# A decoder layer on one core: the pool mixer's bias for half of the token tiles is added by accumulating transfers instead of products

## The chip, the cores and the metric

The kernel runs on one core of one Trainium2 chip. The metric is the time on the device in microseconds (us). A core has five engines that run at the same time, each its own instructions in order: TensorE (PE in the profile, with weight loads as PEld), VectorE (DVE), ScalarE (ACT), GpSimd (POOL) and SyncE (SP). Transfers between memories are issued by an engine and carried out by 16 DMA engines; those that GpSimd issues are queue q0 of the profile, those that SyncE issues are q1. GpSimd's transfers can also add what they bring to what stands at the destination; such a transfer is called accumulating here.

## The reference

One layer with the mixer of kind 0 is computed, for 1024 tokens and a width of 1024, all in float32:

```python
h = rms_norm(x, norm_mix_g)
y = pool_mixer(h, pool_w, pool_b, pool_scale)
x = x + y
f = conv_ffn(rms_norm(x, norm_ffn_g), ffn_w_in, ffn_conv_w, ffn_conv_b, ffn_w_out)
x = x + f
```

`pool_mixer` subtracts h from causal means over 2, 4, 8 and 16 tokens (one window for each quarter of the columns), multiplies each quarter by its own 256 x 256 weights, adds the bias `pool_b` and multiplies by `pool_scale`, one number a column. So the term `pool_scale * pool_b` is one row of 1024 numbers that is added to every token. `conv_ffn` multiplies by a 1024 x 5632 matrix, convolves over three tokens, gates, and multiplies by a 2816 x 1024 matrix.

## The kernel before

**Mixer.** The 1024 tokens are eight tiles j = 0 to 7 of 128 tokens (one a partition) by 1024 columns. For each tile, `rstd_of` on ScalarE takes the norm (`junk_a`, line 178), VectorE scales the band matrix with it (`bandr`, line 187), and TensorE makes the window sums out of the tile as it was loaded (`psd`, line 201). VectorE adds the part that comes from the tile before (line 270), ScalarE copies the result into SBUF as `dh` (line 271), and TensorE multiplies it by the pool's weights, which already hold gain and scale (`psy`, line 286). The bias follows as two products with ones into the same bank (line 289): `bias_hl` holds the bias row, split into two float32r parts in its first two partitions and zero elsewhere, and `ones` is a 128 x 128 tile of ones. VectorE adds the tile `xs[j]` to the bank (line 292), in place, which gives the tile after the mixer, x1; SyncE stores it to `x1_dram`. Its norm follows (`junk_b`), VectorE makes the normed tile `n` (line 304), and TensorE transposes it (`pst`, line 319) into the operand of the feed-forward part. The PSUM banks of `psd`, `psy` and `pst` come from one pool of three, in the order of their use.

**Feed-forward.** Both large products are done by a scheme of seven half-size products (P1 to P7, `STEPS` at line 405), each made from sums and differences of quarters of the operands, and each operand is split into two float32r parts by ScalarE and VectorE (`split`, lines 91 and 92). For a column tile n, `load_in` brings 128 x 2048 numbers `win n` with the quarters a11, a12, a21 and a22. Four sums of the quarters are operands: S1 = a21 + a22 in the place of a21, S2 = a11 + S1 in that of a11, S4 = a12 + S2 in that of a12, and S3 = a11 + a21 in a tile of its own, for which SyncE loads a11 a second time (line 366). Where time allows, `sums_in` makes these by accumulating transfers on GpSimd's queue (line 361); for the column tiles 0 and 1 it makes all four so, during the mixer.

**Order.** The order on each engine is written out by hand: the loop at line 527 runs the tiles in a skewed way (in pass j the norm of tile j, the windows of tile j - 1, the output of tile j - 2, the transposes of tile j - 4), and `issue_after` puts an instruction behind another on its engine. It starts the first products of the feed-forward part among the last tiles. Every engine, GpSimd's queue too, takes its instructions strictly in that order, so a transfer whose wait isn't over holds up all that are behind it.

The loop's passes call these for the sums of column tiles 0 and 1:

```python
if j in (4, 6):
    load_in(j // 2 - 2)
    sums_in(j // 2 - 2, 0)
...
if j in (7, 8):
    sums_in(j - 7, 1)
```

Of the kernel before, what the change touches and what calls it, by code (L numbers as in the profile page):

```python
# [7 lines left out]
F32 = mybir.dt.float32  # L8
# [3 lines left out]
ALU = mybir.AluOpType  # L12
PSUM = bass.MemoryType.PSUM

P = 128
S = 1024
D = 1024
# [22 lines left out]
NOPS_A = 3  # L40

XBUFS = 5

PAD = 24

# [18 lines left out]
def trunk_kernel(ctx: ExitStack, tc: tile.TileContext, x, consts, par, rows, pool_w, w_in, w_out, out):  # L64
    nc = tc.nc

    const = ctx.enter_context(tc.tile_pool(name="const", bufs=1))
    dram = ctx.enter_context(tc.tile_pool(name="dram", bufs=1, space=bass.MemoryType.DRAM))
# [4 lines left out]
    work = ctx.enter_context(tc.tile_pool(name="work", bufs=1, side="right"))  # L73
# [6 lines left out]
    def bank2(name):  # L80
        return ps_p.tile([P, 2 * NH], F32, tag="ps", name=name)
# [16 lines left out]
    xs = {}  # L98

    def load_x(j):  # L100
        if j < 2 or j >= 2 + XBUFS:
            xs[j] = hls.tile([P, D], F32, tag="hl", name=f"x{j}", bufs=7)
        else:
            xs[j] = pp.tile([P, D], F32, tag="x", name=f"x{j}", bufs=XBUFS)
        for cols in HALVES if j == 0 else [slice(0, D)]:
            nc.sync.dma_start(xs[j][:, cols], x[j * P : (j + 1) * P, cols])
# [28 lines left out]
    for g, w in enumerate(WINDOWS):  # L135

        m = band[:, g, :]
# [56 lines left out]
    def mixer_norm(j):  # L194
        t = bands[j] = pp.tile([P, NG, P], F32, tag="bandr", name=f"bandr{j}", bufs=2)
        for groups in [slice(0, 2), slice(2, 4)] if j == 0 else [slice(0, NG)]:
            marks[f"band{j}"] = normed(t[:, groups, :], (band if j else band0)[:, groups, :], stats[j])

    def windows(ps, src, weights):
        for c in range(NK):  # L200
            m = nc.tensor.matmul(ps[:, c * P : (c + 1) * P], src[:, c * P : (c + 1) * P], weights[:, c // 2, :], start=True, stop=True)  # L201
        return m.ins
# [13 lines left out]
    wps = pp.tile([P, 2 * NG, GRP], F32, tag="wps", name="wps")  # L216
# [13 lines left out]


    b8 = rows8[:, 1, :]

    def pool_bias():
        marks["bias"] = nc.scalar.activation(bias8[:, 0, :], b8, AF.Copy).ins
        marks["bias_dve"] = nc.vector.tensor_tensor(bias8[:, 1, :], b8, bias8[:, 0, :].bitcast(F32), ALU.subtract).ins
        for l in range(2):
            m = nc.sync.dma_start(bias_hl[l : l + 1, :].bitcast(F32), bias8[:, l, :].bitcast(F32)).ins
        with tc.issue_after(m):
            for j in range(3, NS):  # L240
                load_x(j)
            nc.sync.dma_start(par_sb[:, :GM], par[:, :GM])
# [14 lines left out]
    def window_sums(j):  # L257
        ps = bank2(f"psd{j}")
        marks[f"psd{j}"] = windows(ps, xs[j], bands.pop(j))
        return ps  # L260

    def mixer_window(j, ps=None):
        ps = window_sums(j) if ps is None else ps
        dh = ds[j] = pp.tile([P, NK, P], F32, tag="dh", name=f"dh{j}", bufs=2)
        ps3 = ps.rearrange("p (c s) -> p c s", c=NK)
        first = ps3[:, :, :HALO]
        if j == 0:
            marks["first"] = nc.vector.tensor_tensor(first, first, fac, ALU.mult).ins
        elif j > 1:
            nc.vector.tensor_tensor(first, first, edges[:, :, j * HALO : (j + 1) * HALO], ALU.add)  # L270
        marks[f"dh{j}"] = nc.scalar.activation(dh, ps3, AF.Copy).ins
# [9 lines left out]
    def mixer_out(j, stats=True):  # L281
        dh = ds.pop(j)
        ps = bank2(f"psy{j}")
        for c in range(NK):
            o = ps[:, c // 2 * GRP : (c // 2 + 1) * GRP]
            nc.tensor.matmul(o, dh[:, c, :], wps[:, c, :], start=c % 4 == 0, stop=False, skip_group_check=True)  # L286
        for h in range(2):
            cols = slice(h * NH, (h + 1) * NH)
            m = nc.tensor.matmul(ps[:, cols], ones, bias_hl[:, cols], start=False, stop=True, skip_group_check=True)  # L289
        marks[f"psy{j}"] = m.ins  # L290
        x1 = n2s[j] = xs.pop(j)
        marks[j] = nc.vector.tensor_tensor(x1, ps, x1, ALU.add).ins
        nc.sync.dma_start(x1_dram[j * P : (j + 1) * P, :], x1)
        if stats:
            mixer_out_stats(j)

    def mixer_out_stats(j):
        n2s[j] = (n2s[j], rstd_of(n2s[j], f"b{j}"))

    def ffn_norm(j):  # L300
        x1, r = n2s[j]
        n2 = n2s[j] = pp.tile([P, D], F32, tag="n2", name=f"n2_{j}", bufs=2)
        nc.vector.tensor_tensor(r[1], r[0], r[1], ALU.mult)
        marks[f"n{j}"] = nc.vector.scalar_tensor_tensor(n2, x1, r[1], gains[0], op0=ALU.mult, op1=ALU.mult).ins
# [10 lines left out]
    def ffn_operand(j):  # L315
        n2 = n2s.pop(j)
        ps = bank2(f"pst{j}")
        for c in range(NK):
            nc.tensor.transpose(ps[:, c * P : (c + 1) * P], n2[:, c * P : (c + 1) * P], ident)  # L319
        ps3 = ps.rearrange("p (c a s) -> p c a s", c=NK, a=2)  # L320
        lo, hi = slice(0, 4), slice(4, 8)
        half, q = divmod(j, NS // 2)
        cols = slice(q * P // 2, (q + 1) * P // 2)
        here, first = (n2f[:, :, h * NH : (h + 1) * NH].rearrange("p c (a s) -> p c a s", a=2)[:, :, :, cols] for h in (half, 0))
        if half == 0:
            split_n(nops["B11"], ps3[:, lo], cols)
            split_n(nops["B21"], ps3[:, hi], cols)
            nc.scalar.activation(here, ps3, AF.Copy)
            return
        b11, b12, b22 = first[:, lo], ps3[:, lo], here[:, hi]  # L330
        nc.scalar.activation(b22, ps3[:, hi], AF.Copy)
        sub(b11, b11, b12)
        marks["T1"] = split_n(nops["T1"], b11, cols)
        sub(here[:, lo], b22, b12)
# [20 lines left out]
    def tmp(name):  # L355
        return work.tile([P, NH], F32, tag="sum", name=name, bufs=3)

    def sums_in(n, step):

        def more(out, a):  # L360
            nc.gpsimd.dma_start(out, a, accum_op=ALU.add)

        a11, a12, a21, a22 = (raws[n][:, i, k * NH : (k + 1) * NH] for i in range(2) for k in range(2))
        if step == 0:
            s3 = sums[n, "S3"] = tmp(f"S3_{n}")
            nc.sync.dma_start(s3, w_in[order[n]][:, 0, :NH])
            more(s3, a21)
            more(a21, a22)
        else:
            sums[n, "S2"] = a11  # L370
            more(a11, a21)
            sums[n, "S4"] = a12
            more(a12, a11)
# [95 lines left out]
    def prep_event(k):  # L469
        if k < len(events):  # L470
            n, p = events[k]
            prep_in(n, STEPS[p][0])
# [49 lines left out]
        mixer_edges()  # L522
    with tc.issue_after(marks["edges_pe"]):
        sums3 = window_sums(3)
    with tc.issue_after(marks["dh1+"]), tc.issue_after(marks["edges"]):
        mixer_out_stats(0)
    for j in range(2, NS + 4):
        if 3 < j < NS:
            with tc.issue_after(marks[1]) if j == 4 else nullcontext():
                mixer_norm(j)  # L530
        if 1 <= j - 1 < NS and j > 2:
            mixer_window(j - 1, {3: sums2, 4: sums3}.get(j))
        if j == NS + 1:
            with tc.issue_after(marks[f"n{NS - 2}"]):
                prep_event(4)
                prep_event(6)
        if 1 <= j - 2 < NS:
            with tc.issue_after(marks["S4", 0] if j == NS + 1 else marks[f"band{min(j, 4)}"]) if j > 2 else nullcontext(), tc.issue_after(marks["psd3"]):
                mixer_out(j - 2)
        if 0 <= j - 2 < NS:  # L540
            with tc.issue_after(marks["dh1+"]):
                ffn_norm(j - 2)
        if 0 <= j - 4 < NS:
            ffn_operand(j - 4)
        if j in (4, 6):
            load_in(j // 2 - 2)
            sums_in(j // 2 - 2, 0)
        if 5 <= j <= 8:
            with tc.issue_after(marks[j - 2]), tc.issue_after(marks[f"b{j - 3}"]):
                prep_event(j - 5)  # L550
        if j in (7, 8):
            sums_in(j - 7, 1)
        if j in (8, 10, 11):
            event((8, 10, 11).index(j))
        with tc.issue_after(marks["edges"]):
            stat(j + 1)
            stat(j + 2)
# [156 lines left out]
    for k in range(-SLOOK, len(oevents)):  # L714
        p, f = oevents[k + SLOOK] if k + SLOOK < len(oevents) else (None, 0)
# [8 lines left out]
        with tc.issue_after(lasts[-1]) if lasts else nullcontext():  # L724
# [12 lines left out]
            p, f = oevents[k]  # L737
# [10 lines left out]
        if f == 0 and opens:  # L748
            for i in range(4):
                tag = ("XXYY" if set_ == "X" else "YZZZ")[i]  # L750
# [15 lines left out]
        for i, g, c, bank in steps:  # L766
            a, b = oops[p, g]
            alone = opens and (p, i) != ("P4", 3)
            for m, (u, v) in enumerate(((0, 0), (0, 1), (1, 0))):
# [3 lines left out]
                    start=opens and first, stop=g == NP2 - 1 and m == 2, skip_group_check=not alone,  # L773
# [83 lines left out]
```

## Time and profile before

| | |
|---|---|
| time, median of 3 runs | 672.28 us (670.89 to 673.64) |
| the profiled execution | 670.79 us, its span 669.0 us |
| TensorE busy | 663.6 us (99%) |
| VectorE busy | 569.1 us (85%) |
| ScalarE busy | 338.8 us (51%) |
| transfers | 101.23 MB, 151 GB/s over the span |
| GpSimd's queue q0 | 12.59 MB |
| granted TensorE clock | 1.000 |

Times are counted from the span's start. The mixer and the start of the feed-forward part lie between 0 and about 90 us. The busy time of an engine is no bound by itself: the chain of waits tells which work ended last at each point. A row of the timeline or of the chain has the start, the length, the engine, the line, the operation with what it writes and reads, and in brackets how long the engine had been idle before and what ended that. Matmul ends are modelled, so that a busy TensorE need not be one that gets its inputs in time. For a DMA row of an engine the length is that of issuing it; the landing is told in the view of transfers.

### The profile page before, as it was taken

How to read it: one execution, taken by the hardware profiler on the slowest of the kernel's cores; microseconds unless marked ns; L12 is line 12 of the kernel's file. 1: busy time of each engine (PE TensorE's matmuls, PEld its weight loads, DVE VectorE, ACT ScalarE, POOL GpSimd, SP SyncE). 2: the span in 40 equal slices, each digit the busy share in tenths (PEclk: the TensorE clock that was granted, in tenths of full speed). 3: DMA queues.
4: the chain of work that ended last, by engine and by line, in shares of the span. 5: the costliest groups of instructions: out<-in, count | busy, mean ns of one | idle time of the engine just before them, and what ended most of it. 6: DMA issues, size and time to landing. Idle time of an engine off the chain costs nothing.

```text
span 669.0 us, 8720 instructions
## 1 busy us (share of the span) xinstructions
PE 663.6 (99%) x3164; PEld 579.2 (87%) x3164; DVE 569.1 (85%) x841; ACT 338.8 (51%) x517; POOL 47.8 (7%) x73
## 2 busy tenths in 40 slices
PE   9999999999999999999999999999999999999997
PEld 7999878888888888888888888888888888888886
DVE  4798999998888888888888888887987988999995
ACT  6696656554544544444544454454554444444441
POOL 3021020111001111111011101100000000000000
PEclk9999999999999999999999999999999999999999
DMA  8983253544444454544444444429999710232231
GB/s 269 326 207 105 85 141 126 167 145 124 133 134 105 123 142 141 143 130 128 135 141 130 113 136 132 111 92 350 332 335 352 269 58 0 62 96 82 62 125 64
DMA packets 41603, 101.23 MB, mean 151 GB/s; under 512 B 4668, under 2 KB 6616, under 8 KB 38744
## 3 DMA queue, kind: packets, MB, share of 16 engines
q1 hardware_dynamic: 34464, 87.55, 37.3%
q0 software_dynamic: 6944, 12.59, 11.3%
q10 hardware_dynamic: 152, 0.53, 0.3%
q8 instruction: 25, 0.41, 0.2%
q14 instruction: 18, 0.15, 0.1%
HBM read 68.14 MB, written 19.92 MB: 132 GB/s over the span
## 4 chain that ended last, share of the span: by engine, by line
PE 96%; DVE 2%; ACT 1%; issue 0%; POOL 0%; ACTq 0%; POOLq 0%
PE oP L771 29%; PE Y L402 25%; PE X L402 17%; PE Z L402 16%; PE psy L286 4%; PE psd L201 2%; PE pst L319 1%; DVE T L339 1%; PE psy L289 1%; PE ps_scale L222 0%; PE idle_ps L149 0%; DVE n2f L580 0%; ACT B L338 0%; PE ps_edges L201 0%; PE ps_gain L248 0%
## 5 line engine op out<-in xcount | busy, mean ns | idle before, releaser
L771 PE MATMUL oP<-oBP,oAP 128*128 128x512 f32 (+1 forms) x924 | 198.9, 378 | 0.1
L771 PEld LDWEIGHTS oP<-oBP,oAP 128*128 128x128 f32 x924 | 174.0, 189 | 25.0 <-DVE oBP L92 0.5
L402 PE MATMUL X<-B,A11s 128*128 128x512 f32 x264 | 61.5, 380 | 0.0
L402 PE MATMUL Y<-T,S3s 128*128 128x512 f32 x264 | 60.8, 380 | 0.4 <-DVE q L431 0.4
L402 PE MATMUL Y<-T,A22s 128*128 128x512 f32 x264 | 60.8, 380 | 0.0
L402 PE MATMUL Z<-T,S1s 128*128 128x512 f32 x264 | 60.8, 379 | 0.0
L402 PE MATMUL X<-B,A12s 128*128 128x512 f32 x264 | 60.6, 379 | 0.0
L402 PE MATMUL Y<-T,S2s 128*128 128x512 f32 x264 | 60.6, 379 | 0.0
L402 PE MATMUL Z<-B,S4s 128*128 128x512 f32 x264 | 60.5, 379 | 0.0
L402 PEld LDWEIGHTS Y<-T,S3s 128*128 128x128 f32 x264 | 49.7, 189 | 8.2 <-DVE q L431 1.2
L402 PEld LDWEIGHTS Y<-T,A22s 128*128 128x128 f32 x264 | 49.7, 189 | 7.9 <-DVE hb L439 0.6
L402 PEld LDWEIGHTS Z<-T,S1s 128*128 128x128 f32 x264 | 49.8, 189 | 7.5 <-DVE T L339 0.4
L402 PEld LDWEIGHTS Z<-B,S4s 128*128 128x128 f32 x264 | 49.8, 189 | 7.3 <-DVE r L436 0.3
L402 PEld LDWEIGHTS Y<-T,S2s 128*128 128x128 f32 x264 | 49.9, 189 | 7.1
L402 PEld LDWEIGHTS X<-B,A11s 128*128 128x128 f32 x264 | 49.7, 189 | 7.3 <-DVE A11s L92 0.4
L402 PEld LDWEIGHTS X<-B,A12s 128*128 128x128 f32 x264 | 49.8, 189 | 7.0
L91 ACT ACTIVATE oBP<-blk 128x512 fp32r<-128x512 f32 x53 | 33.1, 625 | 44.2 <-PE oP L771 30.6
L460 ACT ACTIVATE gate<-gate 128x1024 f32<-128x1024 f32 x22 | 23.2, 1057 | 49.3 <-DVE gate L451 49.3
L91 ACT ACTIVATE oAP<-blk 128x512 fp32r<-128x512 f32 x55 | 34.1, 620 | 19.3 <-DVE blk L350 16.8
L92 DVE TENSOR_TENSOR oBP<-blk,oBP 128x512 fp32r<-128x512 f32 x53 | 36.5, 688 | 8.6 <-ACT oBP L91 6.6
L92 DVE TENSOR_TENSOR oAP<-blk,oAP 128x512 fp32r<-128x512 f32 x55 | 37.7, 685 | 2.6 <-ACT oAP L91 2.6
L450 DVE SCALAR_TENSOR_TENSOR val<-ha,par_sb,val 128x1023 f32<-128x1023 f32 x22 | 28.2, 1283 | 13.2 <-ACT val L449 13.2
(131 smaller groups left out, 958.3 us busy)
## 6 DMA issues: line engine op xcount, KB each, us to landing
win<-in_w_in_dram SPq DMA_DIRECT2D x22, 1024.0 KB, 4.8
g_dram<-val SPq DMA_DIRECT2D x22, 512.0 KB, 2.6
blk<-g_dram SPq DMA_DIRECT2D x33, 256.0 KB, 5.2
blk<-in_w_out_dram SPq DMA_DIRECT2D x31, 256.0 KB, 5.7
win<-win POOLq DMA_DIRECT2D x26, 256.0 KB, 3.5
S<-in_w_in_dram SPq DMA_DIRECT2D x22, 256.0 KB, 3.5
S<-win POOLq DMA_DIRECT2D x22, 256.0 KB, 4.2
A12s<-g_dram SPq DMA_DIRECT2D x22, 256.0 KB, 5.2
```

What stands on the lines that cost most here:

```text
L91: nc.scalar.activation(t[:, 0, :], src, AF.Copy)
L92: m = nc.vector.tensor_tensor(t[:, 1, :], src, t[:, 0, :].bitcast(F32), ALU.subtract)
L201: m = nc.tensor.matmul(ps[:, c * P : (c + 1) * P], src[:, c * P : (c + 1) * P], weights[:, c // 2, :], start=True, stop=True)
L286: nc.tensor.matmul(o, dh[:, c, :], wps[:, c, :], start=c % 4 == 0, stop=False, skip_group_check=True)
L289: m = nc.tensor.matmul(ps[:, cols], ones, bias_hl[:, cols], start=False, stop=True, skip_group_check=True)
L319: nc.tensor.transpose(ps[:, c * P : (c + 1) * P], n2[:, c * P : (c + 1) * P], ident)
L339: return hi, nc.vector.tensor_tensor(l, src, h.bitcast(F32), ALU.subtract).ins
L402: nc.tensor.matmul(bank, a[:, i, ks], woven(b[:, l, k, :]), start=opens and m == 0, stop=m == 11, skip_group_check=not opens)
L450: nc.vector.scalar_tensor_tensor(t[:, 1:], src[:, : S - 1], w[1], t[:, 1:], op0=ALU.mult, op1=ALU.add)
L460: nc.scalar.activation(gate, gate, AF.Silu)
L771: nc.tensor.matmul(bank, a[:, u, i * P : (i + 1) * P], woven(b[:, v, :])[:, c.start // 2 : c.stop // 2, :], start=opens and first, stop=g ...
```

## The change

For the token tiles 4 to 7 the two products with ones are left out. In their place the bias row is added to the residual tile `xs[j]` itself, before line 292 (307 in the changed kernel) reads it:

- `pool_bias` also sends the scaled bias, 8 x 128 numbers, to a row `bias_row` in DRAM, by GpSimd's queue;
- `bias_spread` reads that row back into all 128 partitions of a new tile `bias_b` (512 KB). It has the buffer that `x_edge` had, so it waits until `ps_edges` is made; later `ha0` of the feed-forward part gets the same buffer;
- `bias_into(j)`, called after the windows of tile j, is an accumulating transfer of 512 KB from `bias_b` into `xs[j]`. It waits until TensorE has read `xs[j]` for `psd`, and line 307 waits for it;
- for column tiles 0 and 1, the sum S1 (a21 += a22) is taken out of `sums_in`'s first step into a step of its own, put behind the transfers into `xs[4]` and `xs[5]`.

```diff
+BY_DMA = 4
...
+    bias_row = dram.tile([1, D], F32, tag="bias_row", name="bias_row")
+    biased = {}
+
+    def bias_spread():
+        biased["tile"] = work.tile([P, D], F32, tag="ha", name="bias_b", bufs=1)
+        nc.gpsimd.dma_start(biased["tile"], bias_row.to_broadcast([P, D]))
+
+    def bias_into(j):
+        if j >= BY_DMA:
+            biased[j] = nc.gpsimd.dma_start(xs[j], biased["tile"], accum_op=ALU.add).ins
...
+        nc.gpsimd.dma_start(bias_row.rearrange("o (k p) -> (o k) p", p=P), b8)
...
-            nc.tensor.matmul(o, dh[:, c, :], wps[:, c, :], start=c % 4 == 0, stop=False, skip_group_check=True)
-        for h in range(2):
+            m = nc.tensor.matmul(
+                o, dh[:, c, :], wps[:, c, :], start=c % 4 == 0, stop=j >= BY_DMA and c % 4 == 3, skip_group_check=True
+            )
+        for h in range(0 if j >= BY_DMA else 2):
...
             more(s3, a21)
+        if step == 0 and n > 1 or step == 2:
             more(a21, a22)
-        else:
+        if step == 1:
...
     with tc.issue_after(marks["edges_pe"]):
         sums3 = window_sums(3)
+        bias_spread()
...
             mixer_window(j - 1, {3: sums2, 4: sums3}.get(j))
+            bias_into(j - 1)
...
+        if j in (5, 6):
+            with tc.issue_after(biased[j - 1]):
+                sums_in(j - 5, 2)
```

GpSimd's queue, from its first accumulating transfer on, before (`S3_n` is the tile of the sum S3 of column tile n; `win` written from `win` is, in this order, a21 of column tile 0, a21 of 1, a11 of 0, a11 of 1, a12 of 0, a12 of 1):

```order
L361 DMA S3_0_427<-win0_425 128x512
L361 DMA win0_425<-win0_425 128x512
L361 DMA S3_1_552<-win1_550 128x512
L361 DMA win1_550<-win1_550 128x512
L361 DMA win0_425<-win0_425 128x512
L361 DMA win1_550<-win1_550 128x512
L361 DMA win0_425<-win0_425 128x512
L361 DMA win1_550<-win1_550 128x512
```

And now (`win` from `win` is a21 of 0, a11 of 0, then a21 and a11 of 1, a12 of 0, a12 of 1):

```order
L240 DMA bias_b_335<-bias_row_152 128x1024
L376 DMA S3_0_431<-win0_429 128x512
L244 DMA x4_229<-bias_b_335 128x1024
L376 DMA win0_429<-win0_429 128x512
L376 DMA S3_1_556<-win1_554 128x512
L376 DMA win0_429<-win0_429 128x512
L244 DMA x5_231<-bias_b_335 128x1024
L376 DMA win1_554<-win1_554 128x512 x2
L244 DMA x6_233<-bias_b_335 128x1024
L376 DMA win0_429<-win0_429 128x512
L244 DMA x7_235<-bias_b_335 128x1024
L376 DMA win1_554<-win1_554 128x512
```

The four transfers into x4 to x7 stand among the sums of column tiles 0 and 1, and a21 of column tile 1 has moved behind a11 of column tile 0 and x5.

TensorE from the output product of tile 6 to the transposes of tile 6, before:

```order
L286 MATMUL psy6_627<-wps_151,dh6_570 128x256 x8
L289 MATMUL psy6_627<-bias_hl_100,ones_148 128x512 x2
L319 MATMUL pst4_650<-cst_81,n2_4_533 128x128 x8
L402 MATMUL X0_669<-B11_154,A11s_0_489 128x512 x12
L286 MATMUL psy7_690<-wps_151,dh7_624 128x256 x8
L289 MATMUL psy7_690<-bias_hl_100,ones_148 128x512 x2
L319 MATMUL pst5_713<-cst_81,n2_5_593 128x128 x8
L319 MATMUL pst6_727<-cst_81,n2_6_647 128x128 x8
```

And now:

```order
L299 MATMUL psy6_631<-wps_151,dh6_574 128x256 x8
L334 MATMUL pst4_652<-cst_81,n2_4_537 128x128 x8
L418 MATMUL X0_671<-B11_155,A11s_0_494 128x512 x12
L299 MATMUL psy7_692<-wps_151,dh7_627 128x256 x8
L334 MATMUL pst5_713<-cst_81,n2_5_596 128x128 x8
L334 MATMUL pst6_727<-cst_81,n2_6_649 128x128 x8
```

Only the pairs of products with ones are gone; the rest of TensorE's order is as it was. VectorE and ScalarE have the same instructions, with one or two neighbours of tile 3's and 5's norms exchanged.

## The prediction

> **What bounds the kernel now.** I read the page's head and its chain by engine, then the chain of waits in order of time, then the stretch from 20 to 72 us, where the change is made.
>
> ```profile
> span 669.0 us, 8720 instructions
> PE 663.6 (99%) x3164; PEld 579.2 (87%) x3164; DVE 569.1 (85%) x841; ACT 338.8 (51%) x517; POOL 47.8 (7%) x73
> PE 96%; DVE 2%; ACT 1%; issue 0%; POOL 0%; ACTq 0%; POOLq 0%
> ```
>
> The chain lies on TensorE (PE) for 96% of the span. In order of time (start, length, what) it stays there through the whole mixer:
>
> ```profile
> 18.79 1.79 PE ps_edges L201 x16
> ...
> 31.30 1.79 PE psd L201 x16
> ...
> 43.30 0.46 PE psy L289 x2
> 43.77 0.87 PE pst L319 x8
> 44.64 1.89 PE psd L201 x16
> ...
> 63.94 0.46 PE psy L289 x2
> 64.41 1.75 PE pst L319 x16
> 66.15 5.40 PE X L402 x25
> ...
> 71.58 1.08 PE pst L319 x8
> ```
>
> So a product taken away in the mixer shortens the end, as long as nothing else becomes late. What can become late is seen on the other engines. I write x1_j for the residual add of token tile j (line 292, tile `x`), n_j for its norm (line 304).
>
> ```profile
> 43.40 1.02 ACT L271 ACTIVATE dh<-psd 128x1024 f32<-128x1024 f32 x1
> 50.48 1.22 DVE L292 TENSOR_TENSOR x<-psy,x 128x1024 f32<-128x1024 f32 x1 [0.30 <-PE psy L289]
> 57.06 1.22 DVE L292 TENSOR_TENSOR x<-psy,x 128x1024 f32<-128x1024 f32 x1 [0.96 <-PE psy L289]
> 64.44 1.22 DVE L292 TENSOR_TENSOR x<-psy,x 128x1024 f32<-128x1024 f32 x1 [0.53 <-PE psy L289]
> 56.47 0.64 ACT L91 ACTIVATE S4s<-win 128x512 fp32r<-128x512 f32 x1
> 57.94 0.60 ACT L331 ACTIVATE n2f<-pst 128x512 f32<-128x512 f32 x1 [0.83 <-PE pst L319]
> 58.43 1.06 ACT L178 ACTIVATE junk_b<-x 128x1024 bf16<-128x1024 f32 x1
> 61.43 1.28 DVE L304 SCALAR_TENSOR_TENSOR n<-x,st_b,gain_b 128x1024 f32<-128x1024 f32 x1
> 63.24 0.68 DVE L92 TENSOR_TENSOR S4s<-win,S4s 128x512 fp32r<-128x512 f32 x1
> ```
>
> The adds x1_5, x1_6 and x1_7 wait for TensorE alone, and by under 1 us: VectorE (DVE) is itself almost full here. The slack between n_6 and its transpose is small: n_6 ends at 62.7, and the second half of the transposes that start at 64.41 needs it at about 65.3.
>
> **Removed.** Four pairs of products with ones. The chain charges each pair 0.46 us, so 4 x 0.46 = 1.84 us. Tile 4's share is probably lost at once: the `psd` that follows it (44.64 in the chain, tile 6) takes 1.89 us instead of 1.79, because its bank is only just free: ScalarE (ACT) empties it into `dh` until 43.40 + 1.02 = 44.42, and ScalarE does not get faster. That leaves 3 x 0.46 = 1.4 us. The bounds are 0 (all of it lost in waits) and the eight products' own durations, 8 x 0.488 = 3.9 us, since the ends of matmuls are modelled:
>
> ```profile
> L289 PE MATMUL psy<-bias_hl,ones x16: 392/488/582, 16.2 to 64.0; 128*128 128x512 f32 x16
> ```
>
> **Added.** Six transfers on GpSimd's queue. `bias_row` (4 KB) is sent as soon as the scaled bias is there, long before it is read; I cost it at nothing, and if that cover were gone it would delay only `bias_b`. `bias_b` (512 KB) cannot go before 20.6, when TensorE has finished `ps_edges` and frees its buffer. Then come four accumulating transfers of 512 KB, x4 to x7, one ahead of each residual add. They go into a queue that is in order and had this before, all of it waiting inside:
>
> ```profile
> 30.19 0.89 POOL L361 DMA_DIRECT2D S<-win  x1 [22.98 <-DMA S<-in_w_in_dram]
> 35.43 0.87 POOL L361 DMA_DIRECT2D win<-win  x1 [4.34 <-DVE st_b L182]
> 38.02 0.85 POOL L361 DMA_DIRECT2D S<-win  x1 [1.72 <-PE pst L319]
> 42.10 1.74 POOL L361 DMA_DIRECT2D win<-win  x2 [3.22 <-DMA S<-win]
> 46.67 0.85 POOL L361 DMA_DIRECT2D win<-win  x1 [2.84 <-DVE A11s L92]
> 52.60 0.86 POOL L361 DMA_DIRECT2D win<-win  x1 [5.07 <-DVE A12s L92]
> ```
>
> With the changed order, what stands ahead of what is: S3_0, x4, a21_0, S3_1, a11_0, x5, a21_1, a11_1, x6, a12_0, x7, a12_1 (a21_n is `win n`'s quarter a21, and so on; a11_n adds a21_n, so it waits until a21_n has landed, and everything behind it on GpSimd waits too).
>
> **What an accumulating transfer costs.** From the table of queues: q0, which is GpSimd's, and q1, which is SyncE's (SP):
>
> ```profile
> q1 hardware_dynamic: 34464, 87.55, 37.3%
> q0 software_dynamic: 6944, 12.59, 11.3%
> win<-win POOLq DMA_DIRECT2D x1, 256.0 KB, 3.3
> S<-win POOLq DMA_DIRECT2D x1, 256.0 KB, 3.4
> ```
>
> q0 moved 48 accumulating transfers of 256 KB in 11.3% of 669 us, 75.6 us of all 16 engines: 1.57 us each. q1 moved 87.55 MB in 249.5 us: 1.5 us for 512 KB. The last two rows are single accumulating transfers, issued at 52.60 and at 38.02, with little beside them: 3.3 and 3.4 us from issue to landing. The windows (length, busy times by engine, granted clock, then share of the DMA engines and GB/s) show the same:
>
> ```profile
> 20.00:42.30 22.30, 22.30 (x137) 20.15 (x136) 17.51 (x46) 17.61 (x33) 2.82 (x4) 1.00 0.94 296
> 42.30:43.50 1.20, 1.20 (x7) 1.05 (x6) 1.20 (x2) 1.20 (x5) 1.20 (x2) 1.00 0.00 0
> 43.50:46.40 2.90, 2.90 (x27) 2.74 (x26) 2.73 (x7) 2.51 (x5) 0.34 (x1) 1.00 1.06 180
> 46.40:48.00 1.60, 1.60 (x10) 1.42 (x9) 1.30 (x4) 1.55 (x5) 0.85 (x1) 1.00 0.84 329
> ```
>
> From 43.5 to 46.4 two accumulating transfers keep the engines full at 180 GB/s; the store of x1_4 behind them runs at 329. So 512 KB accumulated costs between 1.5 us (as any transfer) and 3.1 us (twice the 256 KB). No row has this size; it is the same operation as the 1.57 us rows with longer rows per partition, so I take 3.1.
>
> **When x5 lands.** From 20.0 to 42.3 the engines were busy for 0.94 x 22.3 = 21.0 us. Ahead of x5's end there now also stand `bias_b` (1.5), x4 (3.1), a11_0 (1.6, formerly after 42.3), x5 itself (3.1), and a share of the store of x1_4 (0.8 to 1.5). Sum 31.1 to 31.8 us: the last packet at 51.1 to 51.8 if the engines are never idle, about 52.3 with half a microsecond to land and some gaps. x1_5 ran at 50.48 and would now be ready at about 49.6: x5 is late. (x4 can be issued at 33.1, when `psd` of tile 4 ends. Even if SyncE's queue takes every second packet, S3_0 and x4 are through at 33 + 2 x (1.6 + 3.1) = 42.4, before x1_4 wants x4 near 44.5.)
>
> **When x6 lands.** Behind x5's packets come a21_1 (1.6); then 0.7 until a11_1 is issued (S3_1's, issued at 38.02, landed 3.4 us later, at 41.4, and its follower went at 42.10); a11_1's 3.3 to its landing; and x6's 3.1 behind it: 8.7 us after x5, at about 61.0. The adds x1_5 and x1_6 lay only 6.6 us apart, so the lateness grows. a12_0 comes behind x6, at 62.6.
>
> **Who waits for that.** x1_6, 61.0 instead of 57.06. On ScalarE, S4s of column tile 0 (56.47) needs a12_0 and goes at about 62.7; `n2f` and tile 6's statistics (`junk_b`, 58.43) stand behind it, at 63.7, 5.3 us late; n_6 with them, at 66.7. On VectorE 2.5 us of work lie between the start of n_6 and the end of S4s (61.43 to 63.92), so x1_7 begins at 69.2 instead of 64.44. From there to the last transposes (71.58) VectorE is nearly full, so these are 4.8 us late; TensorE has emptied its queue of other work and stands. It has 1.84 us less work, but that only makes it stand longer.
>
> ```profile
> 60.00:70.00 10.00, 10.00 (x56) 8.91 (x55) 9.34 (x21) 5.97 (x13) 0.04 (x1) 1.00 0.32 95
> ```
>
> In this window VectorE, the third busy time, works 9.34 of 10 us.
>
> **The sum.** With x6 at 61.0, +4.8 us. With 2.3 us for each 512 KB, x5 lands at 50.7, x6 at 58.6: +2.4. With more gaps, x6 at 62: +5.8. I take +4.2, nearer to the row's price. The profiled execution took 670.8 us (span 669.0), so 675.0 by it; the median of the runs, 672.28, is 1.5 us above that execution, and the same addition there gives 676.5. I write 676.0. About 0.5% (3.4 us) is what a measurement of this kernel can tell from no change.
>
> **Rivals.**
> A, on time (0.22). If 512 KB cost 1.5 us, the sum for x5 is 21.0 + 1.5 + 1.5 + 1.6 + 1.5 + 0.8 = 27.9, landing at 48.4, and x6 follows 7.1 later at 55.5: both before their adds (49.6 and 56.2). Then 1.4 to 1.84 us are gained: 670.4 to 670.9 by the median. Against it stands the 180 GB/s row. The Trainium skill, DMA: Bandwidth & Descriptors, section on the anatomy of one DMA on the SWDGE path, speaks for this rival: it fits a transfer of GpSimd's queue as 2.0 us plus bytes over 436 GB/s, an estimate of 3.2 us for 512 KB and 2.6 for 256 KB; the trace has 3.3 for the accumulated 256 KB, so the rule is already short there.
> B, late but mostly absorbed (0.13). x6 comes at about 57 to 58; the 0.96 and 0.53 us that VectorE sat idle and n_6's slack swallow it, and the removed products pay the rest: -1 to +2, 671.3 to 674.3. It decides if the engines overlap packets of the two queues better than their shares show.
> C, worse (0.06). x7 becomes the last: with stores beside it x7 lands over 8 us after x6, past 69.2, and column tile 1's sums behind it too: +7 to +9, 679 to 681.
> D, faster (0.04). The products are worth their own 3.9 us and nothing is late: 668.4.
>
> **Chances.** The forecast (late by 2.2 to 5.8 us, 674.5 to 678.1) has 0.55, of which 0.43 beyond 3.4 us. Slower: 0.43 + C's 0.06 = 0.49. Same: 0.12 + A + B = 0.47. Faster: D, 0.04. The range, 670.2 to 678.6, takes in A, B and the forecast.
>
> **What would show it.** Right: x1_5 and above all x1_6 wait for a DMA of `x`, not for TensorE; ScalarE waits for a DMA before S4s of column tile 0; over 3 us of TensorE's idle time between 52 and 78; the landing of the 512 KB accumulating transfers at 5 us and more. Wrong: a landing near 3.5 us; all four adds waiting for TensorE; idle time of TensorE in this stretch unchanged.

## The result, and the profile after

| | before | after |
|---|---|---|
| time, median of 6 runs each | 671.18 us (670.77 to 673.64) | 676.03 us (675.07 to 677.27) |
| ratio, with its 95% interval | | 1.0066 [1.0048, 1.0084] |
| the profiled execution's span | 669.0 us | 674.2 us |
| GpSimd's queue q0 | 12.59 MB | 15.22 MB |

The change makes the kernel slower by 0.66%, some 4.4 us (0.0066 x 671.2), 3.2 to 5.6 us by the interval. The medians lie 4.85 us apart, the profiled spans 5.2 us. (Before is 671.18 us by six runs; the three that the prediction had are among them.) First, from the changed kernel's page, the busy times and the chain by engine:

```profile
PE 662.9 (98%) x3156; PEld 577.8 (86%) x3156; DVE 569.3 (84%) x841; ACT 338.9 (50%) x517; POOL 52.2 (8%) x79
PE 88%; DVE 4%; DMA 4%; ACT 2%; issue 1%; POOL 0%; SPq 0%; ACTq 0%; DVEq 0%; POOLq 0%
```

TensorE is busy for 0.7 us less in a span that is 5.2 us longer, and its share of the chain falls from 96% to 88%: transfers, ScalarE and VectorE now set the end for a while. The timeline of the changed kernel shows where. The first row is a11_0, the second x5; `x<-psy,x` on DVE is x1_5, x1_6, x1_7; S4s is that of column tile 0.

```profile
44.70 0.85 POOL L376 DMA_DIRECT2D win<-win  x1 [4.79 <-DMA win<-win]
45.24 1.19 POOL L244 DMA_DIRECT2D x<-bias_b  x1
52.07 1.23 DVE L307 TENSOR_TENSOR x<-psy,x 128x1024 f32<-128x1024 f32 x1 [2.71 <-DMA x<-bias_b]
60.94 1.22 DVE L307 TENSOR_TENSOR x<-psy,x 128x1024 f32<-128x1024 f32 x1 [3.26 <-DMA x<-bias_b]
63.35 0.63 ACT L93 ACTIVATE S4s<-win 128x512 fp32r<-128x512 f32 x1 [5.17 <-DMA win<-win]
68.73 1.57 PE L334 MATMUL pst<-cst,n 128*128 128x128 f32 x8 [3.87 <-DVE n L319]
69.71 1.22 DVE L307 TENSOR_TENSOR x<-psy,x 128x1024 f32<-128x1024 f32 x1
69.96 4.11 PE L418 MATMUL X<-B,A11s 128*128 128x512 f32 x12
76.79 1.07 PE L334 MATMUL pst<-cst,n 128*128 128x128 f32 x8
```

x1_5 and x1_6 wait for their transfers of the bias. ScalarE waits 5.17 us for a12_0 before S4s of column tile 0; it ran that at 56.47 before. TensorE stands 3.87 us before tile 6's transposes, and the last transposes come at 76.79 instead of 71.58, 5.2 us later: the whole difference of the spans is made by then. The chain of waits names the way:

```profile
46.13 7.19 DMA win<-win
...
53.85 0.52 POOL win L376
54.39 0.54 POOL x L244
54.92 8.40 DMA win<-win
...
63.35 0.63 ACT S4s L93
63.98 0.48 ACT n2f L346
64.47 1.04 ACT junk_b L180 x2
...
67.30 1.30 DVE n L319
...
68.73 1.57 PE pst L334 x8
```

The piece at 54.92 is a12_0, which landed 8.40 us after its issue; before, it was issued at 52.60 and landed after 3.3 us. So it comes late for two reasons: 2.3 us by its issue, some 5 us by its way through the full DMA engines. Its issue hangs on a21_1 (the first row), for whose landing a11_1 waits, with x6 and a12_0 behind it. From a12_0 the chain goes over ScalarE's S4s, `n2f` and tile 6's statistics to n_6 and tile 6's transposes. The add x1_6 isn't on it, though x6's packets, ahead of a12_0's in the queue, are part of those 8.40 us. The windows of the changed kernel (the last three columns are the granted clock, the share of the DMA engines and GB/s) show the transfers in that stretch:

```profile
42.00:46.00 4.00, 3.92 (x29) 3.25 (x28) 3.83 (x8) 3.61 (x6) 1.30 (x2) 1.00 0.58 142
46.00:52.00 6.00, 6.00 (x40) 5.46 (x39) 3.21 (x8) 4.16 (x8) 1.30 (x2) 1.00 1.05 236
52.00:58.00 6.00, 4.76 (x27) 4.16 (x26) 5.21 (x10) 4.62 (x8) 3.52 (x4) 1.00 0.82 190
58.00:64.00 6.00, 6.00 (x30) 5.24 (x29) 1.82 (x2) 0.83 (x3) 0.86 (x1) 1.00 1.06 209
```

The DMA engines are full from 46 to 52 and from 58 to 64, but not between. By windows of half a microsecond they are full until 43.5 and only 0.27 busy from there to 46: a11_0 waited until 44.70 for a21_0's landing (the 4.79 us above), x5 stood behind it, and the packets of both move only from about 46 on. They are idle once more from 53 to 54: a11_1 had waited 6.55 us, until 53.85, for a21_1's landing, with x6 behind it.

### The profile page after: what moved, and what is told of

It reads as the page before. It is cut to its first block, busy times and chain, and to the rows that moved or that the text cites. A ratio compares the mean times of both kernels' runs of the same rounds, so it can differ in the third digit from the quotient of the medians.

```text
span 674.2 us, 8722 instructions
## 1 busy us (share of the span) xinstructions
PE 662.9 (98%) x3156; PEld 577.8 (86%) x3156; DVE 569.3 (84%) x841; ACT 338.9 (50%) x517; POOL 52.2 (8%) x79
## 3 DMA queue, kind: packets, MB, share of 16 engines
q0 software_dynamic: 7696, 15.22, 13.0%
## 4 chain that ended last, share of the span: by engine, by line
PE 88%; DVE 4%; DMA 4%; ACT 2%; issue 1%; POOL 0%; SPq 0%; ACTq 0%; DVEq 0%; POOLq 0%
PE oP L792 29%; PE Y L418 25%; PE X L418 16%; PE Z L418 15%; DMA win<-win 2%; DMA x_dram<-x 1%; PE psd L203 1%; DMA cst<-in_consts_dram 1%; ACT junk_b L180 1%; DVE n L319 1%; DVE x L307 1%; DVE T L354 1%; PE psy L299 1%; PE pst L334 0%; ACT B L353 0%
## 5 line engine op out<-in xcount | busy, mean ns | idle before, releaser
L418 PE MATMUL Y<-T,A22s 128*128 128x512 f32 x264 | 60.9, 380 | 0.0
```

The source lines that it names most:

```text
L418: nc.tensor.matmul(bank, a[:, i, ks], woven(b[:, l, k, :]), start=opens and m == 0, stop=m == 11, skip_group_check=not opens)
```

## The experiments

Each run below was compared with the kernel before on the same chip, in five rounds; the first row repeats the change's own comparison. The differences below are the ratio less one, times the median of before in that comparison. Where an expectation quotes an earlier run, it quotes the difference of medians, which lies up to 0.5 us off (+4.9 for the change, +5.6, +3.7, +1.2).

| run | ratio [95% interval] | difference |
|---|---|---|
| the change | 1.0066 [1.0048, 1.0084] | +4.4 us |
| no products, no transfers for tiles 4 to 7 | 0.9985 [0.9976, 0.9994] | -1.0 us |
| plain copies in place of accumulating | 1.0018 [1.0009, 1.0028] | +1.2 us |
| without a12_0 and a12_1 | 1.0053 [1.0041, 1.0066] | +3.6 us |
| x5 to x7 sent aside | 1.0081 [1.0068, 1.0093] | +5.4 us |
| both of these | 0.9971 [0.9960, 0.9983] | -1.9 us |
| the change, other order of the queue | 1.0021 [1.0012, 1.0030] | +1.4 us |
| tiles 5 to 7, the sums' old order | 1.0035 [1.0022, 1.0048] | +2.3 us |
| tiles 5 to 7, x5 and x6 earlier | 1.0008 [0.9999, 1.0017] | +0.5 us |
| tiles 6 and 7 | 0.9996 [0.9987, 1.0005] | -0.3 us |
| tile 7 alone | 0.9989 [0.9980, 0.9998] | -0.7 us |

### What the removal alone is worth

```diff
-        nc.gpsimd.dma_start(bias_row.rearrange("o (k p) -> (o k) p", p=P), b8)
...
-        bias_spread()
...
-            bias_into(j - 1)
...
-        if step == 0 and n > 1 or step == 2:
+        if step == 0:
             more(a21, a22)
...
-        if j in (5, 6):
-            with tc.issue_after(biased[j - 1]):
-                sums_in(j - 5, 2)
```

> The products with ones of tiles 4 to 7 are taken away and nothing is put in their place: no bias row in DRAM, no spread bias, no transfers of it, and the accumulating sums of the weight tiles in the order that they had before. The bias of token tiles 4 to 7 is left out. My theory: the removal alone is worth three pairs of 0.46 us, so -1.4 us against the kernel before (-0.2%); all of what the change costs comes from the transfers. Rival 1, the products were hidden anyway: 0.0 us. Rival 2, they are worth their own durations: -3.9 us (-0.6%).

Measured: -1.0 us, -1.6 to -0.4 by the interval. That holds the expected -1.4 and leaves out both rivals, 0 and -3.9. The profile's own numbers agree: the chain of this kernel reaches the last transposes at 70.07, 1.51 us earlier than before, and the span is 1.5 us shorter.

```profile
64.65 5.40 PE X L417 x25
...
70.07 1.08 PE pst L333 x8
```

So the products were on the path, at about the price that the chain gave them less tile 4's. That tile 4's is mostly lost is seen too: from the windows (`psd`) of tile 5 to those of tile 6, with tile 4's output between them, TensorE took 6.68 us before and 6.57 here; from those of tile 6 to those of tile 7, with tile 5's output, 6.67 and 6.22. Everything else in the result, some 5.4 us, is the doing of the transfers and of the order of the queue, which this run puts back too.

### The price of accumulating

```diff
-            biased[j] = nc.gpsimd.dma_start(xs[j], biased["tile"], accum_op=ALU.add).ins
+            biased[j] = nc.gpsimd.dma_start(xs[j], biased["tile"]).ins
```

> The change, but x4 to x7 are plain copies of the spread bias instead of accumulating transfers: same bytes, same places in the queues, same waits. They write over the residual x of tiles 4 to 7, which is therefore left out of the result. My theory: what hurts is the price of accumulating; at 1.2 to 1.6 us less for each transfer x5 lands 2.4 to 3.2 us earlier than the 52.0 us of the changed kernel, at 49 to 49.6, and x6 3.6 to 4.8 us earlier than 60.9, at 56 to 57.3. The time is then -1.4 to +0.5 us against the kernel before, 4 to 6 us below the changed kernel. Rival, the order and the waits within the queue hurt and not the price: x6 still lands after 59 and the time stays at +3 us or more.

Measured: +1.2 us (0.6 to 1.9), about 3 us below the change, but not a gain. That lies above the range that I expected and below the rival's. The table of queues, first of the changed kernel, then of this one:

```profile
q0 software_dynamic: 7696, 15.22, 13.0%
```

```profile
q0 software_dynamic: 7696, 15.22, 12.3%
57.51 1.23 DVE L307 TENSOR_TENSOR x<-psy,x 128x1024 f32<-128x1024 f32 x1 [1.46 <-DMA x<-bias_b]
60.07 0.63 ACT L93 ACTIVATE S4s<-win 128x512 fp32r<-128x512 f32 x1 [3.54 <-DMA win<-win]
```

q0 took 13.0% of 674.2 us, 87.6 us of all 16 engines, in the change; 12.3% of 670.9, 82.5 us, here; 75.6 us before. The five plain transfers added 6.9 us, 1.4 each. The four accumulating ones cost 87.6 - 75.6 - 1.4 = 10.6 us, 2.7 each: 1.3 us more than a plain one (the shares are rounded to 0.1%, 0.7 us, so each price is good to some 0.2; that the spread row `bias_b` costs as much as a copy is assumed). Two and three accumulating transfers, in runs further down, give 2.6 and 2.8 in the same way. But even at 1.4 us x6 is 1.46 us late, and a12_0, behind x6, 3.54 us late for ScalarE. So at a plain copy's price some 3 us of the loss are gone. This isn't a share that another order would leave standing: the run with another order, below, gains as much at the full price.

### Two ways, cut one at a time

The first run leaves out a12_0 and a12_1, so that S4s of column tile 0 has nothing to wait for. In the second, the transfers for tiles 5 to 7 keep their places in the queue but write to dead tiles, so that the residual adds have nothing to wait for. The third does both.

```diff
             sums[n, "S4"] = a12
-            more(a12, a11)
```

> The change, without the two accumulating sums a12_0 and a12_1 of column tiles 0 and 1 (their part of the result is left out), so that S4s of column tile 0 has no transfer behind x6 to wait for. My theory has two ways by which x6 is late: x1_6 waits for x6 itself, and ScalarE waits for a12_0 behind x6 with tile 6's statistics queued behind it. Without the second way n_6 is ready about 2 us earlier and the time is about +3 us against the kernel before instead of +4.9. Rival 1, the residual adds' wait alone sets the end: no difference to the changed kernel (+4.9). Rival 2, a12_0's wait alone sets it: the kernel before and below it (0 to -1.4 us).

```diff
+    def aside(j):
+        biased[j] = nc.gpsimd.dma_start(kept[j - 3], biased["tile"], accum_op=ALU.add).ins
...
-        if j >= BY_DMA:
+        if j == BY_DMA:
...
-        x1 = n2s[j] = xs.pop(j)
+        x1 = n2s[j] = kept[j] = xs.pop(j)
```

> The change with the same queue in the same order, but the three transfers of the bias for tiles 5, 6 and 7 go into dead x tiles (of tiles 2, 3 and 4) that nobody reads again. The bias of tiles 5 to 7 is left out. The residual adds then wait for no transfer, while a11_0, a21_1, a11_1, a12_0 and a12_1 are as late as in the change. My theory: ScalarE's wait for a12_0 (landing at about 62.6 us) still makes n_6 late by 4 to 5 us, and the time is +4 to +5 us against the kernel before, within 1 us of the changed kernel. Rival, the wait of x1_5 and x1_6 is what sets the end: the time falls to between -1.4 and +1 us against the kernel before.

> Both cuts at once: the transfers of the bias for tiles 5 to 7 go into dead x tiles, as in the run that sent them aside, and the sums a12_0 and a12_1 are left out, as in the run without them. The bias of tiles 5 to 7 and the two sums are left out of the result. The queue still moves the same bytes up to x7, and TensorE still has none of the products. My theory: the wait of the residual adds and the wait of S4s of column tile 0 are two parallel ways that each cost most of what is lost (+5.6 us with the second alone, +3.7 us with the first alone), and nothing else is lost: with both cut, the time is that of the kernel without products and without transfers, -1.1 us against the kernel before (between -1.6 and -0.4). Rival, the crowd on the DMA engines also slows something else (the stores, the loads of the weight tiles): +0.5 us or more.

Measured: +3.6 us (2.7 to 4.4) with the adds' wait alone, +5.4 us (4.6 to 6.2) with S4s's wait alone, -1.9 us (-2.7 to -1.1) with neither. Timelines, in this order of the three kernels:

```profile
57.80 0.63 ACT L93 ACTIVATE S4s<-win 128x512 fp32r<-128x512 f32 x1
60.59 1.23 DVE L307 TENSOR_TENSOR x<-psy,x 128x1024 f32<-128x1024 f32 x1 [3.17 <-DMA x<-bias_b]
64.96 1.28 DVE L319 SCALAR_TENSOR_TENSOR n<-x,st_b,gain_b 128x1024 f32<-128x1024 f32 x1
74.44 1.06 PE L334 MATMUL pst<-cst,n 128*128 128x128 f32 x8 [1.59 <-DVE n L319]
```

```profile
56.12 1.23 DVE L310 TENSOR_TENSOR x<-psy,x 128x1024 f32<-128x1024 f32 x1 [0.50 <-PE psy L302]
63.10 0.63 ACT L93 ACTIVATE S4s<-win 128x512 fp32r<-128x512 f32 x1 [6.99 <-DMA win<-win]
67.05 1.28 DVE L322 SCALAR_TENSOR_TENSOR n<-x,st_b,gain_b 128x1024 f32<-128x1024 f32 x1
76.53 1.07 PE L337 MATMUL pst<-cst,n 128*128 128x128 f32 x8
```

```profile
55.54 0.64 ACT L93 ACTIVATE S4s<-win 128x512 fp32r<-128x512 f32 x1
69.71 1.06 PE L337 MATMUL pst<-cst,n 128*128 128x128 f32 x8
```

In the second kernel x1_6 runs at 56.12, 4.8 us before it did in the change, and it gains nothing: S4s waits 6.99 us, tile 6's statistics stand behind it on ScalarE, and n_6 (67.05) is as late as in the change (67.30). In the first S4s waits for nothing, but x1_6 itself is late, and n_6 comes 2.3 us earlier (64.96). (Single executions start up to 1 us apart, so a difference of some tenths between two timelines says nothing.) So the two waits are parallel ways to n_6; the later one counts, and it is a12_0's. The timelines show this better than the times: +3.6 us has an interval that overlaps the change's own, 3.2 to 5.6. With both cut, the last transposes begin at 69.71, as in the kernel without any transfer (70.07). The rival of the third run, that the crowd on the DMA engines slows something else too, is out: moving the same bytes up to x7 costs nothing when nobody waits for them or behind them. The -1.9 us is a little more than the -1.6 to -0.4 that I had expected; the intervals of this run and of the one without transfers overlap.

### Order and quantity

The change's queue with each a11 sum put behind the next transfer of the bias:

```diff
         if j in (7, 8):
-            sums_in(j - 7, 1)
+            with tc.issue_after(biased[j - 2]):
+                sums_in(j - 7, 1)
```

> The change with the same transfers in another order on GpSimd's queue: each a11 sum now stands behind the next transfer of the bias, so the queue is S3_0, x4, a21_0, S3_1, x5, a21_1, a11_0, x6, a11_1, a12_0, x7, a12_1. In the changed kernel x5 stood behind a11_0, which waited 4.79 us for a21_0's landing, and x6 behind a11_1, which waited 6.55 us; now neither does. Nothing is left out. My theory: the in-order queue's waits make up most of the lateness; x5 comes about 4 us earlier (48 us, in time) and x6 at about 54 to 56 (in time), while a12_0 stays at 58 to 60 and is still 2 to 3 us late for S4s of column tile 0. The time is -0.5 to +2 us against the kernel before. Rival, the DMA engines are simply too full between 20 and 64 us and the order doesn't matter: +4 us or more, as the changed kernel.

Measured: +1.4 us (0.8 to 2.0), within the forecast and some 3 us below the change, by moving no byte less. x5 is issued at 41.26 instead of 45.24, neither x1_5 nor x1_6 waits for a transfer any more, and what is left is a12_0, 2.21 us late:

```profile
41.26 0.85 POOL L244 DMA_DIRECT2D x<-bias_b  x1 [1.02 <-issue]
50.85 1.23 DVE L307 TENSOR_TENSOR x<-psy,x 128x1024 f32<-128x1024 f32 x1
59.15 0.63 ACT L93 ACTIVATE S4s<-win 128x512 fp32r<-128x512 f32 x1 [2.21 <-DMA win<-win]
```

Then fewer transfers. Three tiles, with the sums in their old order and the transfers between them:

```diff
-BY_DMA = 4
+BY_DMA = 5
...
-        if step == 0 and n > 1 or step == 2:
+        if step == 0:
...
-        if j in (5, 6):
-            with tc.issue_after(biased[j - 1]):
-                sums_in(j - 5, 2)
```

> Tiles 5, 6 and 7 take their bias by accumulating transfers, tile 4 by products again, and the accumulating sums of the weight tiles keep the order that they had before, the transfers standing between them: S3_0, a21_0, S3_1, a21_1, x5, a11_0, a11_1, x6, a12_0, x7, a12_1. Nothing is left out. My theory: what the change cost came from x4 in the full stretch before 42 us and from a11_0 and a11_1 waiting in the queue ahead of the bias. x5 can go with a21_1 at about 42.5 and lands at about 48 (wanted at 49.9); x6 goes at about 47.5 and lands at about 53 (wanted at 56.0); a12_0 behind it lands at about 56.5, 0.6 us late; so the time is -1.1 to +0.5 us against the kernel before. Rival, a 512 KB accumulating transfer in front of a12_0 delays S4s of column tile 0 whatever the order: +2 us or more.

Measured: +2.3 us (1.5 to 3.2). This expectation failed, and the number is the rival's; that it is so "whatever the order" the next run refutes. I had let x5 go at 42.5; it stands behind a21_1, which waited for S3_1's landing until 44.39, and it landed 7 us after its issue:

```profile
44.39 0.86 POOL L376 DMA_DIRECT2D win<-win  x1 [4.91 <-DMA S<-win]
44.97 1.17 POOL L244 DMA_DIRECT2D x<-bias_b  x1
51.91 1.23 DVE L307 TENSOR_TENSOR x<-psy,x 128x1024 f32<-128x1024 f32 x1 [1.85 <-DMA x<-bias_b]
60.70 0.63 ACT L93 ACTIVATE S4s<-win 128x512 fp32r<-128x512 f32 x1 [2.69 <-DMA win<-win]
```

So x5 was moved one place forward and x6 ahead of a11_1, as in the other order, still without x4:

```diff
-BY_DMA = 4
+BY_DMA = 5
...
-        if step == 0 and n > 1 or step == 2:
+        if step == 0 and n != 1 or step == 2:
...
-        if j in (5, 6):
-            with tc.issue_after(biased[j - 1]):
-                sums_in(j - 5, 2)
+        if j == 6:
+            with tc.issue_after(biased[5]):
+                sums_in(1, 2)
...
-            sums_in(j - 7, 1)
+            with tc.issue_after(biased[j - 2]):
+                sums_in(j - 7, 1)
```

> Tiles 5 to 7 by transfers and tile 4 by products, as in the run with the sums' old order (+2.3 us), but x5 stands one place earlier, ahead of a21_1, and x6 ahead of a11_1: S3_0, a21_0, S3_1, x5, a21_1, a11_0, x6, a11_1, a12_0, x7, a12_1. It is the run with another order (+1.2 us) without x4. Nothing is left out. My theory: x5 no longer waits behind a21_1 for S3_1's landing and is in time, as it was with the other order; x4's 2.7 us of all engines are gone, so that a12_0, which came 2.2 us late for S4s there, comes at most 0.5 us late. The time is -0.9 to +0.3 us against the kernel before. Rival, a12_0 waits for the landing of a11_0 behind x5 whatever stands ahead: +1 us or more, as with x4.

Measured: +0.5 us (-0.1 to +1.1), at the upper edge of the forecast. x5 is in time again, but a12_0 is still 2.11 us late, not 0.5: it goes at 51.70, even 0.9 us earlier than before the change, but lands 6.1 us after that and not 3.3, while the DMA engines are full from 46 to 58 (the last two rows, from the windows). That x4 is gone, and tile 4's products are back, is worth 0.9 us against the run with the other order (their intervals overlap a little), though it takes nothing from a12_0's lateness.

```profile
49.59 1.21 DVE L307 TENSOR_TENSOR x<-psy,x 128x1024 f32<-128x1024 f32 x1
57.79 0.64 ACT L93 ACTIVATE S4s<-win 128x512 fp32r<-128x512 f32 x1 [2.11 <-DMA win<-win]
46.00:52.00 6.00, 6.00 (x42) 5.54 (x41) 5.59 (x11) 5.20 (x10) 2.03 (x3) 1.00 1.08 239
52.00:58.00 6.00, 6.00 (x34) 5.35 (x33) 4.67 (x10) 3.88 (x8) 1.72 (x3) 1.00 1.07 235
```

Last, two tiles and one, both with the sums in their old order (`BY_DMA = 6` and `BY_DMA = 7`, otherwise the diff of the first run with three tiles):

> As the run with tiles 5 to 7, but tiles 6 and 7 alone by transfers. Without x5 the queue is as before until a11_1 (46.6 us), then x6, a12_0, x7, a12_1; between 46.6 and 52.0 the queue of the kernel before had nothing to do. Nothing is left out. My theory: two pairs of products are gained and nothing is late: -0.7 to -0.9 us against the kernel before. Rival, x6 ahead of a12_0 delays S4s: +1 us or more.

> Tile 7 alone by a transfer, which stands between a12_0 and a12_1 on the queue. Nothing is left out. My theory: one pair of products is gained and nothing is late, -0.4 us against the kernel before, at the edge of what five rounds tell. Rival, a12_1 behind x7 comes too late for S4s of column tile 1 (wanted at 67.8 us): +1 us or more.

Measured: -0.3 us (-0.9 to +0.3) with two, -0.7 us (-1.3 to -0.1) with one. Timelines, of two tiles and of one:

```profile
57.81 0.63 ACT L93 ACTIVATE S4s<-win 128x512 fp32r<-128x512 f32 x1 [1.13 <-DMA win<-win]
71.25 1.06 PE L334 MATMUL pst<-cst,n 128*128 128x128 f32 x8 [0.53 <-DVE n L319]
```

```profile
57.01 0.64 ACT L93 ACTIVATE S4s<-win 128x512 fp32r<-128x512 f32 x1
```

With x6 ahead of it a12_0 landed 5.1 us after its issue, ScalarE waited 1.13 us for it and TensorE 0.53 us for n_7, so "nothing is late" failed there; the time, whose interval takes in the expected -0.7 to -0.9 as well as no gain, can't tell what that cost. x7 stands behind a12_0, which landed after 3.3 us as before the change, and nothing waits; that expectation held, and its rival didn't. Tile 7 alone is the only one of the runs that compute everything whose interval lies below the kernel before and, of these, the fastest; the gain, 0.1%, is too small to tell from no change by the bound of the prediction. Its profiled execution, the longest of the eleven (a span of 669.1 us), doesn't show it.

## Why the prediction was right, step by step

**Removed, 1.4 us.** Right: -1.0 us measured (-1.6 to -0.4), and tile 4's share was mostly lost, 0.11 us of 0.46 left.

**The price, 3.1 us for 512 KB.** Mis-sized: 2.7 us from the queue's share. Doubling the 256 KB row (1.57) overstates it by 0.4 us; the nearest row was still far better than the lower bound, 1.5.

**When x5 lands, 52.3.** It was there by 52.07, for reasons that partly cancel, so this hit is in part luck. The engines were not "never idle": they stood for some 1.8 us between 43.5 and 46, because a11_0 waits on GpSimd for a21_0's landing and x5 stands behind it. I had counted a11_0 as 1.6 us of packets, not as a wait. The transfers were shorter than I took them to be, and the idle stretch made up for it. That this wait matters is what the run with another order shows: x5 went 4 us earlier and was in time.

**When x6 lands, 61.0, and a12_0, 62.6.** They were there by 60.94 and 63.3, and mostly by the steps forecast: a21_1 landed 1.2 us after x5 (forecast 1.6), a11_1 went 0.5 us later (0.7), and from there to x6's landing it took 7.1 us (6.4).

**Who waits.** Right in both places, and the signs named came: x1_5 and x1_6 wait for a DMA of `x`, ScalarE for one before S4s, TensorE stands for 5.1 us between 52 and 78 (1.24 and 3.87), and the 512 KB transfers land 6.5 us and more after their issue. The runs add which of the two counts: a12_0's, whose wait alone costs as much as both; with x6's alone n_6 comes 2.3 us earlier. In the prediction both stood in one line, and n_6 was rightly hung on ScalarE's.

**The end.** n_6 was forecast for 66.7 and began at 67.30; x1_7 came at 69.71 (forecast 69.2; no wait for a transfer in its row), the last transposes 5.2 us late (forecast 4.8). Of the sum, +4.2 us was taken; the ratio gives +4.4, the medians +4.85. That the time itself, written as 676.0, came out at 676.03 is luck: it was counted from a median of 672.28, which six runs put at 671.18, so it stood for a loss of 3.7 us.

**Rival A** (1.5 us a transfer, so all is on time and 1.4 to 1.84 us are gained) is refuted twice: by the price, and by the run with plain copies, in which 1.4 us a transfer still left a12_0 3.54 us late and the kernel 1.2 us slower. Its working had only the landings of x5 and x6 and left out a12_0 behind them. B fell with x6's landing at 60.9 instead of 57 to 58. C didn't happen: the add x1_7 waits for no transfer. D (3.9 us for the products) fell with the first run.

## What to carry to other kernels

Before work is moved from the busiest engine to a queue, price it in time of all DMA engines, and look at what stands behind it: here 0.46 us of TensorE for each tile was paid with 2.7 us of all 16 engines, in front of a sum that another engine was about to read. The consumer to watch is the first instruction that waits on its in-order engine, with all that is queued behind it, and not only the reader of the tile that was touched. Where two waits lead to the same instruction, cutting one shows little; cut each alone and both together.

## What was not expected of the hardware

After TensorE's 3.87 us of idle time the granted clock fell to a half. The windows of the changed kernel:

```profile
68.00:70.00 2.00, 1.27 (x9) 1.30 (x9) 2.00 (x4) 0.00 (x0) 0.00 (x0) 0.79 0.00 0
70.00:72.00 2.00, 2.00 (x7) 1.64 (x6) 2.00 (x3) 1.04 (x2) 0.00 (x0) 0.50 0.13 53
```

And the timeline and a window of the run with plain copies:

```profile
65.46 1.06 PE L334 MATMUL pst<-cst,n 128*128 128x128 f32 x8 [2.04 <-DVE n L319]
66.28 4.52 PE L418 MATMUL X<-B,A11s 128*128 128x512 f32 x12
68.00:70.00 2.00, 2.00 (x6) 1.59 (x5) 2.00 (x5) 2.00 (x5) 0.00 (x0) 0.50 0.64 262
```

Twelve products of column tile 1 took 4.11 us in the change and 4.52 us here, where the kernel without transfers took 2.84 us for twelve such. In the change the dip cost nearly nothing: its last transposes start at 76.79, and n_7, begun at 75.36 and 1.28 us long, was ready only at about 76.6. Nor do its executions show a clear price: with a mean clock of 0.997 four spans are 673.4 to 674.4 us, with 1.000 one is 674.3 (the sixth, at 0.995, is 675.6). With plain copies, three of the eleven executions had a mean clock of 0.997 or less, with spans of 670.9 to 671.8 us, and the others 668.8 to 670.5 us; whether the dip makes these three longer, or a longer wait makes both, no run settles. The Trainium skill, TensorE: Matmul & The Clock Gate, section on HAM oscillation, names gaps of more than about 3.4 us as those after which the clock is taken down. The 3.87 us agree with it, and so do the 4.60 us of the run with x5 to x7 sent aside, after which the clock was at 0.50 too. With plain copies the idle time before the dip was 2.04 us (eight transposes ran between the two), so here a shorter one was enough. In the run without a12_0 and a12_1, whose idle times there were 1.79 and 1.59 us, the clock stayed at 1.000.

Accumulating was the other size that I didn't know: 512 KB took 2.7 us of all 16 engines accumulated and 1.4 us copied, by the two queue shares above.
